# Latent attention: the 64 sample queries of two heads in one tile of 128 rows

## The chip, the cores and the metric

The kernel runs on one core of one Trainium2 chip. The metric is the device time of one execution in microseconds (us); for one core, the time of that core. The engines are TensorE (PE; its weight loads have a line of their own, PEld), VectorE (DVE), ScalarE (ACT), GpSimd (POOL) and SyncE (SP), which here only issues loads.

## What is computed

One step of a two-layer encoder over two groups of tokens: a prompt of 256 new tokens with no past, and a sample of 64 new tokens behind a cache of 128. D_MODEL is 2048, all in float32. The first layer mixes by latent attention (16 heads), the second by stick-breaking attention (16 heads); each layer is `x + W_o(mixer(RMSNorm(x)) * silu(gate))`, and a final norm follows. The change touches only the first layer's attention:

```
proj = h @ w_in                      # query latent, kv latent, rotary key, gate
q = (rms(cq) @ w_q_up): 128 plain + 64 rotary columns a head
kv = ckv_all @ w_kv_up               # per head 128 of k, 128 of v
k = [k plain, one rotary key shared by all heads]
s = q.k * 192**-0.5; masked where key chunk > query chunk (64 frames)
o = softmax(s) @ v
out = (o * silu(gate)) @ w_o
```

A sample query sees the 128 cached keys and the sample's own 64: 192 keys. A prompt query sees the prompt's keys up to the end of its own chunk: the first 128 queries at most 128 keys, the next 128 up to 256.

## The kernel before, in words

All 320 new tokens (T = 320: 256 of the prompt, then 64 of the sample, `S`) are columns of one activation, and KV = 448 adds the 128 of the cache. Weight products are made from fp32r halves: `split` (L67) casts a loaded weight tile to `hi` on ScalarE and subtracts to `lo` on VectorE, and each product is taken as hi·hi + hi·lo + lo·hi, three matmuls. `plain_split` (L148) does the same to an activation. Where a product is small, plain fp32 is used: TensorE then shows two passes for one product, with two weight loads.

The layer's input products and gates come first (to L319). Then the attention stage (L321 to L486) takes the heads in eight pairs. A pair runs: in every other pair (`even`) the rotary query products of four heads (L410 to L419); two plain query products (L423); two key products of 448 columns (L432); the rotary halves of the query, `qr`, `QA` (high and low part in one tile) and `QB` (high part with four mask rows) (L441 to L451); and four groups that make the pair's V for tokens 128 to 255, 0 to 127, the sample's own and the cache (L458 to L479). The sample's own V group has high and low latent in one 128-row tile, `own`, and adds the two halves of the result (`low`, L474).

Then the pair's heads each go through three steps, which `mla_head` (L340) returns:
- `scores` (L345): queries are the weights that stay in the array, keys stream. Prompt queries 0 to 127 against 128 keys, queries 128 to 255 against 256 keys, both into `sc`, and the sample's 64 queries against 192 keys into 64 rows of `o`. The latter are five products: three for the plain part (L358 to L360), `QA` and `QB` (L361, L362). Then for each part the maximum (L373), the exponential with its row sum (L374), reciprocals (L375, L376) and a scale (L378); p is the prompt's probabilities, `pq` the sample's.
- `transposes` (L381): five transposes into one bank `tr`; the sample's 192 columns are taken as columns 0 to 127 and 64 to 191, and `pq` has 64 rows of zeros. The first 256 columns are split into `ph`, `pl`, the others copied as `pt`.
- `values` (L394): three fp32r products for the prompt's first 128 keys (L396 to L398), then fp32 ones: keys 128 to 255 (L399), the cache's 128 keys for the sample (L400), the sample's own (L401, whose `vv` has 64 rows of zeros). The result times the gate (L403) is split into `oh`, `ol` for the output product.

The order of the work is written by hand through a queue of steps: behind each product group stands a `tick` (L61) that runs the next entry. A pair's scores of both heads are issued at once behind its V groups, and L486 queues the rest for the following groups: two empty entries, the first head's transposes, an empty one, the second head's transposes, the first head's values, the second's. So the first transposes stand behind three product groups of the next pair. After the last pair three first halves of the output product (`gemms`, L104) take the place of those groups. Within an engine's queue, instructions that are ready may have been put ahead of others when the program was built. Buffers that matter: PSUM banks `sc` 2, `o` 2, `tr` 1, `g` 3; `whi`/`wlo` 3; `QA` 4; `qr`, `og` 1.

Of the kernel before, what the change touches and what calls it, by code (L numbers as in the profile page):

```python
# [17 lines left out]
P = 128  # L18
# [17 lines left out]
def stream_encoder(  # L36
# [136 lines left out]

    def sum_bank():
        return pss.tile([P, 512], F32, name="sc")[:, :T]
# [22 lines left out]
    with ExitStack() as stack:  # L198
        mp = stack.enter_context(tc.tile_pool(name="mla", bufs=1, reuse_waits="tile"))
        with tc.tile_pool(name="mla_a", bufs=1, reuse_waits="tile") as pa:  # L200
# [66 lines left out]
            for j in range(4):  # L267
                QB = mp.tile([P, T], F32R, name=f"QB{j}")
                s.copy(QB[ROPE : ROPE + 4, :], qm[ROPE : ROPE + 4, :])
                QBs.append(QB)  # L270

# [56 lines left out]
        R = slice(0, ROPE + 4)  # L328


        pqs, vvs = [], []
        for i in range(2):
            pq = pb.tile([P, 192], F32, name=f"pq{i}")
            v.memset(pq[TS:P, :], 0.0)
            pqs.append(pq)
            vv = pb.tile([P, 3, 256], F32, name=f"vv{i}")
            v.memset(vv[TS:P, 2, :], 0.0)
            vvs.append(vv)

        def mla_head(h, qn, qh, ql, QA, QB, kn, kh, kl, vh, vl, vv, c0):  # L340

            vs = slice(c0, c0 + P)
            at = {}

            def scores():  # L345
                sc = pss.tile([P, 512], F32, name="sc")
                o = pso.tile([P, 512], F32, name="o")
                for out, q0, q1, k0, k1 in (
                    (sc[:, 0:128], 0, P, 0, P),
                    (sc[:, 128:384], P, TP, 0, TP),  # L350
                    (o[0:TS, T:512], TP, T, TP, KV),
                ):
                    q, k = slice(q0, q1), slice(k0, k1)
                    if q0 == 0:
                        pe.matmul(out, qn[:, q], kn, start=True, stop=False)
                    else:
                        q_ = slice(q0 - P, q1 - P)
                        pe.matmul(out, qh[:, q_], kh[:, k], start=True, stop=False)  # L358
                        pe.matmul(out, qh[:, q_], kl[:, k], start=False, stop=False)
                        pe.matmul(out, ql[:, q_], kh[:, k], start=False, stop=False)  # L360
                    pe.matmul(out, QA[:, q], KA[:, k], start=False, stop=False)  # L361
                    pe.matmul(out, QB[R, q], KB[R, k], start=False, stop=True)  # L362
                nm = pb.tile([P, 4], F32, name="nm", bufs=2)
                sm = pb.tile([P, 4], F32, name="sm", bufs=2)
                p = pb.tile([P, 384], F32, name="p", bufs=2)
                pq = pqs[h % 2]
                parts = (
                    (p[:, 0:128], sc[:, 0:128], P, 0),
                    (p[:, 128:384], sc[:, 128:384], P, 1),
                    (pq[0:TS, :], o[0:TS, T:512], TS, 2),  # L370
                )
                for dst, src, n, i in parts:
                    v.tensor_reduce(out=nm[:n, i : i + 1], in_=src, axis=AX.X, op=ALU.max, negate=True)  # L373
                    s.activation(dst, src, AF.Exp, bias=nm[:n, i : i + 1], accum_out=sm[:n, i : i + 1])  # L374
                v.reciprocal(sm[:, 0:2], sm[:, 0:2])  # L375
                v.reciprocal(sm[:TS, 2:3], sm[:TS, 2:3])  # L376
                for dst, src, n, i in parts:
                    v.tensor_scalar(dst, dst, sm[:n, i : i + 1], None, op0=ALU.mult)  # L378
                at.update(o=o, p=p, pq=pq)

            def transposes():  # L381
                p, pq = at["p"], at["pq"]
                tr = pst.tile([P, 512], F32, name="tr")

                for c, src in ((0, p[:, 0:P]), (P, p[:, P:TP]), (TP, pq[:, 0:P]), (T, pq[:, TS:192]), (384, p[:, TP:384])):
                    pe.transpose(tr[:, c : c + P], src, ident_t)  # L386
                ph = pb.tile([P, TP], F32R, name="ph", bufs=2)
                pl = pb.tile([P, TP], F32R, name="pl", bufs=2)
                plain_split(ph, pl, tr[:, 0:256])
                pt = pb.tile([P, 256], F32, name="pt", bufs=2)  # L390
                s.copy(pt, tr[:, 256:512])
                at.update(ph=ph, pl=pl, pt=pt)

            def values():  # L394
                o, ph, pl, pt = (at[x] for x in ("o", "ph", "pl", "pt"))
# [7 lines left out]
                v.tensor_tensor(out=og, in0=o[:, :T], in1=sg[:, h, :], op=ALU.mult)  # L403
                plain_split(oh[:, h, :], ol[:, h, :], og)
# [3 lines left out]
        for pair in range(H // 2):  # L408
# [13 lines left out]
            heads = []  # L422
            for j in range(2):  # L423
                ps = gemm_lora(whi, wlo, j, cq_h, cq_l, T)
                qn = pb.tile([P, T], F32, name="qn", bufs=2)
                qh = pb.tile([P, T - P], F32R, name="qh", bufs=2)
                ql = pb.tile([P, T - P], F32R, name="ql", bufs=2)
                v.tensor_tensor(out=qn, in0=ps, in1=rq, op=ALU.mult)
                plain_split(qh, ql, qn[:, P:T])
                heads.append([qn, qh, ql])  # L430
            whi, wlo = split(raw[:, 1024:2048], 1024)
            for j in range(2):  # L432
# [6 lines left out]
                heads[j] += [None, None, kn, kh, kl]  # L439
            x1c, x1s, x2c, x2s = ab  # L440
            for j in range(2):  # L441
                i = 2 * (pair % 2) + j
                qr = pb.tile([ROPE, T], F32, name="qr")
                rows = slice(32 * i, 32 * i + 32)
                v.tensor_tensor(out=qr[0:32, :], in0=x1c[rows, :], in1=x2s[rows, :], op=ALU.subtract)
                v.tensor_tensor(out=qr[32:64, :], in0=x1s[rows, :], in1=x2c[rows, :], op=ALU.add)
                QA = pb.tile([P, T], F32R, name="QA", bufs=4)
                s.copy(QA[0:ROPE, :], qr)
                v.tensor_tensor(out=QA[ROPE:P, :], in0=qr, in1=f32(QA[0:ROPE, :]), op=ALU.subtract)
                s.copy(QBs[i][0:ROPE, :], f32(QA[0:ROPE, :]))  # L450
                heads[j][3:5] = [QA, QBs[i]]  # L451
# [5 lines left out]
            vv = vvs[pair % 2]  # L457
            for i, t0 in ((0, P), (None, 0), (2, None), (1, T)):  # L458
# [21 lines left out]
            work = []  # L480
            for j in range(2):
                work.append(mla_head(2 * pair + j, *heads[j], vh, vl, vv, j * P))
            (s0, t0, v0), (s1, t1, v1) = work
# [267 lines left out]
```

## Time and profile before

| | us |
|---|---|
| median of 3 runs (lowest, highest) | 1100.1 (1099.86, 1100.15) |
| the profiled execution | 1099.41 |
| its span, first to last instruction | 1097.6 |
| TensorE busy | 1076.9 |
| VectorE busy | 667.8 |
| ScalarE busy | 578.5 |
| mean granted clock of TensorE, share of full speed | 0.995 |

A row of a profile names line, engine, operation and tiles as out<-in, and its time in us or ns; busy shares count an engine from the start of an instruction to its end, and matmuls overlap each other. A row of the timeline gives the start in us from the first instruction, then the length, and joins equal neighbours (x2). The layer's attention stage lies at about 183 to 370 us.

### The profile page before, as it was taken

The page shows a single profiled execution, that of the slowest core. Times are in us where ns is not written, and L with a number is a line of the kernel's source. Part 1 is how long each engine was busy: PE and PEld are TensorE (multiplying, and loading weights), DVE is VectorE, ACT ScalarE, POOL GpSimd, SP SyncE. Part 2 cuts the span into 40 slices and gives each one's busy share as a digit, 9 for nine tenths or more (in the row PEclk, how much of TensorE's full clock was granted, in tenths as well). Part 3 has the DMA queues.
Part 4 walks back from the last instruction along what each step waited for, and adds up shares of the span by engine and source line. Part 5 has one row for each costly group of instructions (what it writes and reads, how often), then busy time and mean ns, then how long its engine had stood idle before and what let it go on. Part 6 is the DMA issues. An engine that isn't in the chain of part 4 may idle for free.

```text
span 1097.6 us, 18604 instructions
## 1 busy us (share of the span) xinstructions
PE 1076.9 (98%) x7484; PEld 1070.5 (98%) x7484; DVE 667.8 (61%) x1345; ACT 578.5 (53%) x1228; POOL 18.7 (2%) x38
## 2 busy tenths in 40 slices
PE   7999999999999999999999999999999999999994
PEld 7999999999999999999999999999999999999994
DVE  7776556887887555565555555555555555554444
ACT  7755555665656444445455554544555545544441
POOL 0000000000000000000000000000000000000000
PEclk9999999999999999999999999999999999999997
DMA  9545443321322745543435444444444444434422
GB/s 310 167 159 192 154 151 99 116 97 58 116 62 73 236 174 177 174 166 127 161 125 182 133 161 138 165 151 146 133 155 148 145 154 139 157 125 154 153 78 96
DMA packets 30550, 159.39 MB, mean 145 GB/s; under 512 B 4264, under 2 KB 8304, under 8 KB 13952
## 3 DMA queue, kind: packets, MB, share of 16 engines
q1 hardware_dynamic: 26912, 151.01, 40.1%
q0 software_dynamic: 1712, 5.98, 1.5%
q10 hardware_dynamic: 1840, 1.22, 0.4%
q8 instruction: 58, 0.95, 0.4%
q14 instruction: 28, 0.23, 0.1%
HBM read 149.59 MB, written 8.60 MB: 144 GB/s over the span
## 4 chain that ended last, share of the span: by engine, by line
PE 97%; DMA 1%; DVE 1%; ACT 0%; issue 0%; DVEq 0%; SPq 0%
PE g L84 25%; PE g L87 25%; PE g L85 25%; PE g L124 2%; PE g L126 2%; PE g L125 2%; PE g L468 1%; PE g L469 1%; PE g L470 1%; PE tr L386 1%; PE sc L556 1%; DVE x L646 1%; DMA xt<-xT 1%; PE o L580 1%; PE sc L538 1%; PE tr L568 0%
## 5 line engine op out<-in xcount | busy, mean ns | idle before, releaser
L72 ACT CAST whi<-raw 128x512 fp32r<-128x512 f32 (+1 forms) x539 | 309.3, 615 | 328.4 <-PE g L85 254.9
L73 DVE TENSOR_TENSOR wlo<-raw,whi 128x512 fp32r<-128x512 f32 (+1 forms) x539 | 353.1, 682 | 129.8 <-ACT whi L72 116.4
L84 PE MATMUL g<-x2h,whi 128*128 128x320 f32 x1024 | 306.1, 313 | 0.0
L85 PE MATMUL g<-x2l,whi 128*128 128x320 f32 x1024 | 302.2, 309 | 0.0
L84 PE MATMUL g<-ah,whi 128*128 128x320 f32 x848 | 250.8, 310 | 0.0
L85 PE MATMUL g<-al,whi 128*128 128x320 f32 x848 | 250.4, 309 | 0.0
L85 PEld LDWEIGHTS g<-x2l,whi 128*128 128x128 f32 x1024 | 192.5, 188 | 0.0
L84 PEld LDWEIGHTS g<-x2h,whi 128*128 128x128 f32 x1024 | 192.5, 188 | 0.0
L87 PE MATMUL g<-x2h,wlo 128*128 128x320 f32 x1024 | 171.0, 309 | 0.0
L85 PEld LDWEIGHTS g<-al,whi 128*128 128x128 f32 x848 | 159.2, 188 | 0.1
L84 PEld LDWEIGHTS g<-ah,whi 128*128 128x128 f32 x848 | 159.1, 188 | 0.1
L87 PEld LDWEIGHTS g<-x2h,wlo 128*128 128x128 f32 x1024 | 155.4, 188 | 0.0
L87 PE MATMUL g<-ah,wlo 128*128 128x320 f32 x848 | 141.6, 309 | 0.0
L87 PEld LDWEIGHTS g<-ah,wlo 128*128 128x128 f32 x848 | 128.7, 188 | 0.0
L633 DVE TENSOR_TENSOR x<-g,x 128x320 f32<-128x320 f32 x16 | 7.9, 491 | 37.5 <-PE g L87 37.5
L124 PE MATMUL g<-cq_h,whi 128*128 128x320 f32 x96 | 30.1, 314 | 0.0
L125 PE MATMUL g<-cq_l,whi 128*128 128x320 f32 x96 | 29.7, 309 | 0.0
L126 PE MATMUL g<-cq_h,wlo 128*128 128x320 f32 x96 | 29.7, 309 | 0.0
L621 DVE TENSOR_TENSOR g<-g,r 128x320 f32<-128x320 f32 x16 | 7.9, 492 | 34.5 <-PE g L87 34.5
L609 DVE TENSOR_TENSOR kT<-g,r 128x320 f32<-128x320 f32 x16 | 7.9, 491 | 34.0 <-PE g L87 34.0
L468 PE MATMUL g<-whi,ckv_h 128*128 128x256 f32 x96 | 28.3, 295 | 0.0
L603 DVE TENSOR_TENSOR q<-g,r1s 128x320 f32<-128x320 f32 x16 | 7.9, 491 | 32.4 <-PE g L87 32.3
(267 smaller groups left out, 1384.9 us busy)
## 6 DMA issues: line engine op xcount, KB each, us to landing
raw<-wsb SPq DMA_DIRECT2D x64, 1024.0 KB, 4.8
raw<-wo SPq DMA_DIRECT2D x32, 1024.0 KB, 4.9
raw<-win SPq DMA_DIRECT2D x21, 1024.0 KB, 4.9
raw<-wmla SPq DMA_DIRECT2D x12, 1024.0 KB, 4.8
xt<-xT SPq DMA_DIRECT2D x16, 160.0 KB, 2.7
ok<-kT POOLq DMA_DIRECT2D x16, 160.0 KB, 2.4
ov<-vT POOLq DMA_DIRECT2D x16, 160.0 KB, 2.1
raw<-win SPq DMA_DIRECT2D x3, 768.0 KB, 7.4
```

The source lines that it names most:

```text
L72: s.copy(hi[:, c], raw[:, c])
L73: v.tensor_tensor(out=lo[:, c], in0=raw[:, c], in1=f32(hi[:, c]), op=ALU.subtract)
L84: pe.matmul(out, hi[:, w], xh[:, k, :], start=k == 0, stop=False)
L85: pe.matmul(out, hi[:, w], xl[:, k, :], start=False, stop=False)
L87: pe.matmul(out, lo[:, i * P : (i + 1) * P], xh[:, k, :], start=False, stop=k == KT - 1)
L124: pe.matmul(out, hi[:, w], xh[:, k, :n], start=k == 0, stop=False)
L125: pe.matmul(out, hi[:, w], xl[:, k, :n], start=False, stop=False)
L126: pe.matmul(out, lo[:, w], xh[:, k, :n], start=False, stop=k == LT - 1)
L386: pe.transpose(tr[:, c : c + P], src, ident_t)
L468: pe.matmul(out, ckv_h[:, k, ts], whi[:, w], start=k == 0, stop=False)
L469: pe.matmul(out, ckv_l[:, k, ts], whi[:, w], start=False, stop=False)
L470: pe.matmul(out, ckv_h[:, k, ts], wlo[:, w], start=False, stop=k == LT - 1)
```

## The change

Scores, softmax and transposes are written for a pair of heads rather than for a head. The sample's 64 queries of head 0 are rows 0 to 63 and those of head 1 rows 64 to 127 of one tile. For that `qh`, `ql` become fixed tiles with 256 columns whose last 128 hold the sample's queries and, at the other head's place, zeros that are written once; `QA`, `QB` and `qr` hold both heads (640 columns, ordered so that the two sample ranges are neighbours: `pair_columns`). The sample's probabilities on the sample's own keys are written as a block diagonal into the right half of `pq`, so that one product with `vo` (own V of head 0 in rows 0 to 63, of head 1 in rows 64 to 127) serves both heads; those on the cached keys are the left half. Head 0's fourth transpose takes the left half, head 1's the right. The sample's values of both heads, their gate product and split come at the end of head 1's `values`. The queue of steps keeps its entries.

```diff
+    def pair_columns():
+
+        return (slice(0, T), slice(0, T)), (slice(T, T + TS), slice(TP, T)), (slice(T + TS, 2 * T), slice(0, TP))
...
-            for j in range(4):
-                QB = mp.tile([P, T], F32R, name=f"QB{j}")
-                s.copy(QB[ROPE : ROPE + 4, :], qm[ROPE : ROPE + 4, :])
+            for j in range(2):
+                QB = mp.tile([P, 2 * T], F32R, name=f"QB{j}")
+                for c, src in pair_columns():
+                    s.copy(QB[ROPE : ROPE + 4, c], qm[ROPE : ROPE + 4, src])
...
+        qss = []
         for i in range(2):
...
+            q_ = [pb.tile([P, 2 * P], F32R, name=f"q{n}{i}") for n in ("h", "l")]
+            zero = slice(192 - TS * i, TP - TS * i)
+            for t in q_:
+                s.activation(t[:, zero], ident_t[:, :TS], AF.Copy, scale=0.0)
+            qss.append(q_)
+
+        pq = pb.tile([P, 2 * P], F32, name="pq")
+        v.memset(pq[:, P:], 0.0)
+
+        def mla_pair(pair, qns, QA, QB, ks, vh, vl, vv, vo):
+
+            at = [{}, {}]
 
             def scores():
...
+                    for out, q, n in ((sc[:, 0:P], slice(0, P), P), (sc[:, P:384], slice(P, TP), TP)):
+                        if n == P:
+                            pe.matmul(out, qns[j][:, q], kn, start=True, stop=False)
+                        else:
+                            pe.matmul(out, qh[:, 0:P], kh[:, 0:TP], start=True, stop=False)
+                            pe.matmul(out, qh[:, 0:P], kl[:, 0:TP], start=False, stop=False)
+                            pe.matmul(out, ql[:, 0:P], kh[:, 0:TP], start=False, stop=False)
+                        q = slice(q.start + j * (T + TS), q.stop + j * (T + TS))
+                        pe.matmul(out, QA[:, q], KA[:, 0:n], start=False, stop=False)
+                        pe.matmul(out, QB[R, q], KB[R, 0:n], start=False, stop=True)
...
+                out = os[:, T:512]
+                for j in range(2):
+                    _, kh, kl = ks[j]
+                    qh, ql = qss[j]
+                    for q_, k_ in ((qh, kh), (qh, kl), (ql, kh)):
+                        first = j == 0 and k_ is kh and q_ is qh
+                        pe.matmul(out, q_[:, P:], k_[:, TP:KV], start=first, stop=False)
+                both = slice(TP, TP + P)
+                pe.matmul(out, QA[:, both], KA[:, TP:KV], start=False, stop=False)
+                pe.matmul(out, QB[R, both], KB[R, TP:KV], start=False, stop=True)
+                e = mp.tile([P, T], F32, name="sil")[:, :192]
...
+                for dst, src, nm, sm in parts:
+                    v.tensor_reduce(out=nm, in_=src, axis=AX.X, op=ALU.max, negate=True)
+                    s.activation(dst, src, AF.Exp, bias=nm, accum_out=sm)
+                for dst, src, nm, sm in parts:
+                    v.reciprocal(sm, sm)
+                    if dst is not e:
+                        v.tensor_scalar(dst, dst, sm, None, op0=ALU.mult)
+                v.tensor_scalar(pq[:, 0:P], e[:, TS:], sm, None, op0=ALU.mult)
+                for j in range(2):
+                    rows = slice(TS * j, TS * j + TS)
+                    v.tensor_scalar(pq[rows, P + TS * j : P + TS * j + TS], e[rows, 0:TS], sm[rows], None, op0=ALU.mult)
+
+            def transposes(j):
+                p = at[j]["p"]
                 tr = pst.tile([P, 512], F32, name="tr")
+                more = pq[:, j * P : (j + 1) * P]
+                for i, src in enumerate((p[:, 0:P], p[:, P:TP], p[:, TP:384], more)):
+                    pe.transpose(tr[:, i * P : (i + 1) * P], src, ident_t)
...
+            def values(j):
...
-                pe.matmul(o[:, P:TP], vv[:, 0, vs], pt[:, 128:256], start=False, stop=True)
-                pe.matmul(o[:, TP:T], vv[:, 1, vs], pt[:, 64:128], start=True, stop=False)
-                pe.matmul(o[:, TP:T], vv[:, 2, vs], pt[:, 0:64], start=False, stop=True)
-                og = pb.tile([P, T], F32, name="og")
...
+                pe.matmul(o[:, P:TP], vv[:, 0, vs], pt[:, 0:P], start=False, stop=True)
+                og = pb.tile([P, TP], F32, name="og")
+                v.tensor_tensor(out=og, in0=o[:, :TP], in1=sg[:, h, :TP], op=ALU.mult)
+                plain_split(oh[:, h, :TP], ol[:, h, :TP], og)
+                if j:
+                    past = at[0]["pt"]
+                    pe.matmul(o[:, TP:384], vo, pt[:, P:], start=True, stop=False)
+                    for i in range(2):
+                        c = slice(i * TS, (i + 1) * TS)
+                        pe.matmul(
+                            o[:, TP + i * TS : TP + (i + 1) * TS], vv[:, 1, i * P : (i + 1) * P],
+                            past[:, P + i * TS : P + (i + 1) * TS], start=False, stop=i == 1,
+                        )
+                    og = pb.tile([P, TP], F32, name="og")[:, :P].rearrange("p (j t) -> p j t", j=2)
+                    both = slice(h - 1, h + 1)
+                    v.tensor_tensor(
+                        out=og, in0=o[:, TP:384].rearrange("p (j t) -> p j t", j=2), in1=sg[:, both, S], op=ALU.mult
+                    )
+                    plain_split(oh[:, both, S], ol[:, both, S], og)
...
-                plain_split(qh, ql, qn[:, P:T])
-                heads.append([qn, qh, ql])
+                qh, ql = qss[j]
+                if j == 0:
+                    plain_split(qh[:, 0:192], ql[:, 0:192], qn[:, P:T])
+                else:
+                    plain_split(qh[:, 0:P], ql[:, 0:P], qn[:, P:TP])
+                    plain_split(qh[:, 192:TP], ql[:, 192:TP], qn[:, S])
...
+            QA = pb.tile([P, 2 * T], F32R, name="QA", bufs=2)
+            QB = QBs[pair % 2]
+            qr = pb.tile([ROPE, 2 * T], F32, name="qr")
+            for i, (c, src) in enumerate(pair_columns()):
+                i = 2 * (pair % 2) + min(i, 1)
                 rows = slice(32 * i, 32 * i + 32)
...
+                v.tensor_tensor(out=qr[0:32, c], in0=x1c[rows, src], in1=x2s[rows, src], op=ALU.subtract)
+                v.tensor_tensor(out=qr[32:64, c], in0=x1s[rows, src], in1=x2c[rows, src], op=ALU.add)
+            s.copy(QA[0:ROPE, :], qr)
+            v.tensor_tensor(out=QA[ROPE:P, :], in0=qr, in1=f32(QA[0:ROPE, :]), op=ALU.subtract)
+            s.copy(QB[0:ROPE, :], f32(QA[0:ROPE, :]))
...
-                    low = pb.tile([TS, 256], F32, name="low")
-                    s.copy(low, out[TS:P, :])
-                    v.tensor_tensor(out=vv[0:TS, i, :], in0=out[0:TS, :], in1=low, op=ALU.add)
+
+                    other = pb.tile([P, P], F32, name="other")
+                    for j in range(2):
+                        rows, rest = slice(TS * j, TS * j + TS), slice(TS - TS * j, P - TS * j)
+                        s.copy(other[rows, :], out[rest, j * P : (j + 1) * P])
+                        v.tensor_tensor(out=vo[rows, :], in0=out[rows, j * P : (j + 1) * P], in1=other[rows, :], op=ALU.add)
...
```

## Rows read from the trace of the kernel before

**Rows 1.** The page's first part: busy us, share of the span, instructions.

```profile
PE 1076.9 (98%) x7484; PEld 1070.5 (98%) x7484; DVE 667.8 (61%) x1345; ACT 578.5 (53%) x1228; POOL 18.7 (2%) x38
```

**Rows 2.** The chain that ended last, by engine.

```profile
PE 97%; DMA 1%; DVE 1%; ACT 0%; issue 0%; DVEq 0%; SPq 0%
```

**Rows 3.** Busy time by stretch: from:to, length, engines, granted clock, DMA share, GB/s.

```profile
310.00:330.00 20.00, 20.00 (x144) 19.59 (x143) 18.34 (x45) 12.07 (x35) 0.00 (x0) 1.00 0.31 95
330.00:353.00 23.00, 23.00 (x179) 22.60 (x178) 17.45 (x46) 15.12 (x44) 0.00 (x0) 1.00 0.22 79
```

**Rows 4.** Line 355, all heads: ns min/median/max, first and last start.

```profile
L355 PE MATMUL sc<-kn,qn x32: 272/275/296, 200.6 to 351.5; 128*128 128x128 f32 x32
```

**Rows 5.** Timeline of TensorE, first and second transposes of a pair.

```profile
315.01 0.38 PE L386 MATMUL tr<-ident_t,p 128*128 128x128 f32 x2
315.23 0.38 PE L386 MATMUL tr<-ident_t,pq 128*128 128x128 f32 x2
...
319.75 0.38 PE L386 MATMUL tr<-ident_t,p 128*128 128x128 f32 x2
```

**Rows 6.** Timeline of TensorE, the fp32 products of one head's values.

```profile
304.61 0.39 PE L399 MATMUL o<-pt,vv 128*128 128x128 f32 x2
304.83 0.33 PE L400 MATMUL o<-pt,vv 128*128 128x64 f32 x2
305.00 0.39 PE L401 MATMUL o<-pt,vv 128*128 128x64 f32 x2
305.19 0.36 PE L468 MATMUL g<-whi,ckv_h 128*128 128x256 f32 x1
305.40 0.28 PE L469 MATMUL g<-whi,ckv_l 128*128 128x256 f32 x1
```

**Rows 7.** Timeline of TensorE's weight loads, the same products.

```profile
304.49 0.31 PEld L399 LDWEIGHTS o<-pt,vv 128*128 128x128 f32 x2
304.72 0.30 PEld L400 LDWEIGHTS o<-pt,vv 128*128 128x128 f32 x2
...
305.17 0.19 PEld L468 LDWEIGHTS g<-whi,ckv_h 128*128 128x128 f32 x1
```

**Rows 8.** Timeline of TensorE: first sample score of a head, and what follows the fifth.

```profile
309.26 0.25 PE L358 MATMUL o<-kh,qh 128*64 128x192 f32 x1
...
309.71 0.33 PE L124 MATMUL g<-cq_h,whi 128*128 128x320 f32 x1
```

**Rows 9.** Timeline of TensorE in the second layer: 192 columns behind 128-column weights.

```profile
498.80 0.25 PE L559 MATMUL sc<-sph,minusR 128*128 128x192 f32 x1
498.89 0.28 PE L559 MATMUL sc<-spl,minusR 128*128 128x192 f32 x1
```

**Rows 10.** Groups of VectorE, 201 to 353 us: busy us, mean ns; idle before.

```profile
L73 DVE TENSOR_TENSOR wlo<-raw,whi 128x512 fp32r<-128x512 f32 x50 | 33.8, 687 | 7.2 <-ACT whi L72 6.4
...
L150 DVE TENSOR_TENSOR ql<-qn,qh 128x192 fp32r<-128x192 f32 x14 | 4.9, 352 | 1.7 <-ACT qh L149 1.7
```

**Rows 11.** Timeline of VectorE through a pair's softmax.

```profile
308.11 0.28 DVE L373 TENSOR_REDUCE nm<-sc 128x1 f32<-128x128 f32 x1
308.41 0.69 DVE L73 TENSOR_TENSOR wlo<-raw,whi 128x512 fp32r<-128x512 f32 x1
...
312.36 0.34 DVE L373 TENSOR_REDUCE nm<-o 64x1 f32<-64x192 f32 x1
...
313.92 0.31 DVE L378 TENSOR_SCALAR pq<-pq,sm 64x192 f32<-64x192 f32 x1
```

**Rows 12.** Timeline of VectorE, the last split of the attention stage.

```profile
369.98 0.49 DVE L150 TENSOR_TENSOR al<-og,ah 128x320 fp32r<-128x320 f32 x1 [0.53 <-ACT ah L149]
```

**Rows 13.** Timeline of ScalarE behind the first transposes of that pair.

```profile
316.88 0.46 ACT L448 CAST QA<-qr 64x320 fp32r<-64x320 f32 x1 [2.38 <-DVE qr L445]
...
317.74 0.36 ACT L149 CAST ph<-tr 128x256 fp32r<-128x256 f32 x1
...
318.86 0.37 ACT L391 COPY pt<-tr 128x256 f32<-128x256 f32 x1 [0.51 <-DVE pl L150]
```

More of the change, by code (lines that the diff above doesn't have):

```diff
@@ L328, in stream_encoder @@
         R = slice(0, ROPE + 4)
-        pqs, vvs = [], []
+        S = slice(TP, T)
+        qss = []
         for i in range(2):
[L333 to L343, printed above, removed]
-            def scores():
[L346 to L382, printed above, removed]
@@ L388, in transposes @@
                 pl = pb.tile([P, TP], F32R, name="pl", bufs=2)
[L389 to L395, printed above, removed]
+                plain_split(ph, pl, tr[:, 0:TP])
+                pt = pb.tile([P, 2 * P], F32, name="pt", bufs=2)
+                s.copy(pt, tr[:, TP:512])
@@ L396, in values @@
+                at[j].update(ph=ph, pl=pl, pt=pt)
+            def values(j):
+                h = 2 * pair + j
+                vs = slice(j * P, (j + 1) * P)
+                if j:
+                    at[1]["o"] = pso.tile([P, 512], F32, name="o")
+                o, ph, pl, pt = (at[j][x] for x in ("o", "ph", "pl", "pt"))
                 pe.matmul(o[:, 0:TP], vh[:, vs], ph, start=True, stop=False)
@@ L421, in stream_encoder @@
             whi, wlo = split(raw[:, 0:1024], 1024)
-            heads = []
+            qns, ks = [], []
             for j in range(2):
@@ L438, in stream_encoder @@
                 s.copy(kn, ps[:, :P])
-                heads[j] += [None, None, kn, kh, kl]
+                ks.append((kn, kh, kl))
             x1c, x1s, x2c, x2s = ab
-            for j in range(2):
-                i = 2 * (pair % 2) + j
-                qr = pb.tile([ROPE, T], F32, name="qr")
-                rows = slice(32 * i, 32 * i + 32)
[L445 to L451, printed above, removed]
+            QA = pb.tile([P, 2 * T], F32R, name="QA", bufs=2)
[3 more added lines that the diff above has]
+                i = 2 * (pair % 2) + min(i, 1)
+                rows = slice(32 * i, 32 * i + 32)
+                v.tensor_tensor(out=qr[0:32, c], in0=x1c[rows, src], in1=x2s[rows, src], op=ALU.subtract)
[3 more added lines that the diff above has]
+            s.copy(QB[0:ROPE, :], f32(QA[0:ROPE, :]))
             if not even:
@@ L456, in stream_encoder @@
             vl = pb.tile([P, 256], F32R, name="vl", bufs=2)
-            vv = vvs[pair % 2]
+            vv = pb.tile([P, 2, 256], F32, name="vv", bufs=2)
+            vo = pb.tile([P, P], F32, name="vo", bufs=2)
             for i, t0 in ((0, P), (None, 0), (2, None), (1, T)):
@@ L473, in stream_encoder @@
                 elif t0 is None:
-                    low = pb.tile([TS, 256], F32, name="low")
-                    s.copy(low, out[TS:P, :])
-                    v.tensor_tensor(out=vv[0:TS, i, :], in0=out[0:TS, :], in1=low, op=ALU.add)
+                    other = pb.tile([P, P], F32, name="other")
+                    for j in range(2):
+                        rows, rest = slice(TS * j, TS * j + TS), slice(TS - TS * j, P - TS * j)
+                        s.copy(other[rows, :], out[rest, j * P : (j + 1) * P])
+                        v.tensor_tensor(out=vo[rows, :], in0=out[rows, j * P : (j + 1) * P], in1=other[rows, :], op=ALU.add)
                 else:
@@ L479, in stream_encoder @@
                 tick()
[L480 to L483, printed above, removed]
-            s0()
-            s1()
+            scores, transposes, values = mla_pair(pair, qns, QA, QB, ks, vh, vl, vv, vo)
+            scores()
+            t0, t1 = partial(transposes, 0), partial(transposes, 1)
+            v0, v1 = partial(values, 0), partial(values, 1)
             steps.extend(([], [], [t0], [], [t1], [v0], [v1]))
```

24 lines of the change are left out of this document (18 added, 6 removed).

## The prediction, made before the changed kernel had run

> **What bounds the kernel now.** I read the page's first part, then the chain that ended last, then busy time by stretch, then TensorE's own order of instructions around a pair of heads. The first says that TensorE works 1076.9 us, 98% of the span [rows 1]. The chain says that 97% of the span is followed back through TensorE alone [rows 2]. A share over the span could hide a stage with another limit, so I looked at the attention stage by itself: in a 20 us stretch that opens with rotary products TensorE is busy 20.00 us, VectorE 18.34, ScalarE 12.07; in the following 23 us TensorE again all of it, VectorE 17.45; the granted clock is 1.00, the 2.4 GHz level [rows 3]. The list of waits has no line for TensorE in this stage. So each TensorE pass that goes is time that goes, as long as VectorE, the next in line, stays hidden. The eight pairs' score blocks begin from 200.6 to 351.5 us [rows 4].
>
> One more reading decides the prices: the duration of a matmul (0.25 to 0.39 us) is a latency; what it costs is the distance from one start to the next.
>
> **Part by part, on TensorE.**
>
> *Transposes.* Before, five per head: three of p, two of the sample's small tile, whose 192 columns were taken as two overlapping slices. After, four. They start 0.22 us apart in twos, 0.11 us each [rows 5]. Two fewer per pair, eight pairs: 2 x 0.11 x 8 = **1.76 us**.
>
> *Values.* Each fp32 product here is two passes. Before, a head has three of them behind its three fp32r products, six passes: two of 128 columns (L399), four of 64 (L400, L401). They run from 304.61 to 305.19, and the product behind them takes 0.21 us to its successor where 0.12 is usual, so the six cost 0.58 + 0.09 = 0.67 us [rows 6]. The weight loads say why: two from 304.49, two from 304.72, two more, and the next at 305.17: 0.68 / 6 = 0.113 us each, whether 128 or 64 columns stream behind [rows 7]. I therefore price a pass at one weight load. After, a pair has two passes for each head's own 128 columns, two for the shared `vo` and two for each head's cached values: ten in place of twelve. 2 x 0.113 x 8 = **1.81 us**. If instead a pass costs what stands between the starts (0.22, 0.17 and 0.19 for the three lines, [rows 6]), a pair goes from 2 x 0.58 = 1.16 to 3 x 0.22 + 0.17 + 0.19 = 1.02, and the term is 0.14 x 8 = 1.1 us. That is its lower end; I take the upper, because the late start behind the group has to be paid somewhere.
>
> *Sample scores.* Before, five 192-column products per head onto 64 rows: 309.26 to 309.71, 0.45 us, 0.90 per pair [rows 8]. After, eight onto 128 rows: each head's three content products stay (the other head's columns are zeros), the two rotary and mask products are shared. No row has a run of 192-column products with 128-column weights. Bounds: L559 is two of that shape in a row, 0.09 us apart [rows 9], which makes 0.72 and a gain of 0.18 x 8 = 1.4 us; the weight loads of [rows 7] follow each other 0.113 apart, which makes 0.90 and no gain. I take **0**: in L559 only one load falls into the short distance, in a run of eight every load does.
>
> *Unchanged there:* the prompt scores, eight products per head, and the four groups that make V.
>
> The sum on TensorE is 1.76 + 1.81 = 3.6 us.
>
> **Beside it, on VectorE and ScalarE.** VectorE's work per pair: one reduction less (six to five), one scale more (six to seven), one reciprocal more, one `ql` more (head 1's low part in two pieces), two rotary pieces more (three ranges of columns, not two), one `QA` fewer but twice as wide, one add more for `vo`, one gate product and one split more for the sample's columns. That is five instructions and a reciprocal more, and some 320 columns fewer, since reductions and scales lose one 64-row tile. From a 192-column and a 512-column row, (687 - 352) / 320 = 1.05 ns a column and 0.15 us fixed [rows 10]: 6 x 0.15 - 0.34 = about +0.56 us. Hidden behind TensorE: 18.34 + 0.56 = 18.9 of the 19.5 us that such a stretch would have, and the next has 5 us free [rows 3]. ScalarE loses one exponential with its accumulator read and two rotary casts and gains four small copies; with 12 of 20 us it is covered too. The setup exchanges four memsets for one memset and four 64-column copies of zeros, in the stage's first microseconds, beside the products ahead of the first scores. Loads and their queues stay as they are.
>
> *The softmax chain.* Its last result is now needed first: the fourth transpose of head 0 reads the pair's sample tile, so it waits for all five parts, both heads. Before, six parts ran in two serial blocks, 308.11 to 313.92 + 0.31 = 314.23 [rows 11], and TensorE came to the first transposes at 315.01 [rows 5], 5.30 us behind the last score product [rows 8]. After, five sixths of 6.1 us end at 313.2 if the parts stay serial. If five independent parts overlap better, the sample's own path sets the end: reduction to last scale took 312.36 to 314.23, 1.9 us [rows 11]; from the last product's end, 309.71 + 0.25, that and two more scales end near 312.3. Cover left: 1.8 to 2.7 us; cost zero. If the cover were gone, TensorE would stand for the overrun in each pair (the third rival). Where the next pair has no rotary products the first transposes also stand behind three groups, one of them wider: more room.
>
> *The end of the stage.* The pair's sample columns come last and share one buffer with head 1's, so a product, a cast and a subtraction more follow in series before k = 14 and 15 of the output product can be read. Before, the last such write ended at 369.98 + 0.49 = 370.47 us [rows 12]. The addition is three instructions of 128 columns, some 0.8 us by the price above; TensorE has the k's of three banks to take meanwhile. So 0 to 0.8 us, and I take 0.2.
>
> So 3.6 - 0.2 = 3.4 us: the profiled execution, 1099.4 us, would be 1096.0, and since the median of the runs is 0.7 us above it, **1096.7 us** there.
>
> The Trainium skill, "TensorE: Matmul & The Clock Gate", section "Back-to-back issue gap", prices a single matmul at N/2.4 ns plus 2.5: 29 ns for 64 columns, 56 for 128, 82.5 for 192. By that rule the edit of the values is worth nothing (4 x 56 + 8 x 29 against 6 x 56 + 4 x 29), the transposes 0.9 and the scores 1.3, an estimate of 2.2 us in all, 1097.9. The spacing of 0.113 us speaks against it [rows 7].
>
> **Rivals.**
>
> *Columns set the price, not weight loads.* Then scores give 1.4, transposes 1.76 (their spacing is a row), values 1.1: 4.3 - 0.2 = 4.1 us, 1096.0. For it: the 0.09 of L559 [rows 9]. Against it: the even weight loads [rows 7]. With scores at that end and values at mine it is 5.0 - 0.2, 1095.3, the lowest that the rows give. Chance 0.10. The skill's gap rule, above, is this mechanism with other numbers.
>
> *A late eviction takes the place of the passes.* In the stretches that open with rotary products ScalarE's cast of the transposed p (317.74) stands behind the rotary casts, which waited 2.38 us for VectorE; the copy of the rest of that bank ends at 319.23 [rows 13], and TensorE needs the bank for head 1's transposes at 319.75 [rows 5]. Room: 0.5 us. With one wide `QA` the cast waits for six rotary pieces rather than two. Four more at about 0.4 us are 1.6, less 1 to 2 us that an earlier end of the softmax may return: the copy is 0 to 1.6 us later, the stall up to 1.1 us in each of three such stretches, 3.3 at most. Taking 2.2, the time is 1098.9. Against it: the order on ScalarE may put the p cast first. Chance 0.18.
>
> *Slower: the whole-pair softmax overtakes its cover.* If VectorE runs other ready work between the parts (it did so once, a 0.69 us split behind the first reduction, [rows 11]), TensorE stands before the first transposes in seven of eight pairs; the last pair has three half products behind it. It decides from 315.0 us on in that stretch, 1.8 us beyond my serial estimate; to be told apart from no change the overrun must exceed (3.4 + 2.2) / 7 = 0.8 us. With 1.2 us it is 7 x 1.2 - 3.4 = +5.0, 1105.1. Against it: four or five such splits would have to come between. Chance 0.08.
>
> *Much less goes than I say:* an order in which the fp32 passes no longer pay for their loads, or stalls of 0.2 us a pair from VectorE's added load; 3.4 less 1.6 is 1.8, 1098.3. Chance 0.09.
>
> **How the numbers follow.** Forecast 0.55, the four cases 0.10, 0.18, 0.08, 0.09. About 0.2%, 2.2 us, is what a measurement can tell from no change: faster means below 1097.9. The forecast, the columns case and a third of the late evictions lie there, 0.71; slower is the one case, 0.08; the rest, 0.21, is the same. The range reaches down to 1095.0, just under the lowest sum, and up to 1099.3; the upper half of the late evictions and the slower case, under 0.2, are left out.
>
> **What would show it.** Right: the distance from the first to the last `sc<-kn,qn`, 150.9 us before [rows 4], shrinks by 7 x 0.45 = 3.1; the sample's products stand 0.11 apart; TensorE still has no line among the waits of this stage. Late evictions: TensorE waits for ScalarE's `pt` or `ph` before the second transposes of a pair. Overtaken cover: it waits for VectorE's `pq` before the first. The sum is wrong if the eight sample products stand 0.09 apart, or if the ten fp32 passes of the values take less than their loads.

## The result, and the profile after

| | before | after |
|---|---|---|
| median of the runs, us | 1100.12 | 1109.65 |
| ratio, 95% interval | | 1.0089 (1.0076 to 1.0101) |
| span of the profiled execution, us | 1097.6 | 1107.2 |
| mean granted clock, share of full speed | 0.995 | 0.991 |

The changed kernel is 9.5 us slower; 3.4 us faster was forecast, with 1095.0 to 1099.3 us as the range. Two runs with a mean granted clock of 0.75 to 0.77 (1298.7 and 1321.3 us) are left out of every median and ratio here. In the rows below, lines are those of the changed kernel: L363 is the first prompt score, L425 the last product of a head's own values, L427 the gate product of its prompt columns, L431 the product with `vo`, L434 the cached values.

First the page's engines (as [rows 1]):

```profile
PE 1076.7 (97%) x7436; PEld 1068.9 (97%) x7436; DVE 672.1 (61%) x1390; ACT 577.5 (52%) x1226; POOL 18.7 (2%) x38
```

48 TensorE instructions are gone, as the sum said, yet its busy time is only 0.2 us less. VectorE has 4.3 us more, 0.54 per pair. Next, the score blocks, first and last start (as [rows 4]):

```profile
L363 PE MATMUL sc<-kn,qn x32: 271/273/275, 201.2 to 361.1; 128*128 128x128 f32 x32
```

From the first to the last it is now 159.9 us against 150.9: 9.0 us of the loss lie there, in the attention stage. Who waited for whom on TensorE, over the whole run (us in total, times, longest), and below it the same for its weight loads:

```profile
PE o L431 <- DVE og L427: 8.5, 4, 2.6
PE o L84 <- ACT whi L72: 7.3, 2, 5.8
PE sc L674 <- ACT sq L684: 1.1, 1, 1.1
```

```profile
PEld o L431 <- DVE og L427: 9.3, 4, 2.8
```

The second and third lines lie at the start and the end of the run, with similar ones before (5.7 and 1.1 us). The first is new: the product with `vo` waits for head 1's gate product, 2.8 us in each of three pairs and 0.9 in one (counted at its weight load; the matmul's own idle time is 0.2 us less). TensorE around one of them:

```profile
239.95 0.38 PE L425 MATMUL o<-pt,vv 128*128 128x128 f32 x2
...
241.00 0.28 PE L512 MATMUL g<-whi,ckv_l 128*128 128x256 f32 x1
243.88 0.49 PE L431 MATMUL o<-pt,vo 128*128 128x128 f32 x2 [2.60 <-DVE og L427]
244.21 0.56 PE L434 MATMUL o<-pt,vv 128*128 128x64 f32 x4
...
245.32 0.41 PE L513 MATMUL g<-wlo,ckv_h 128*128 128x256 f32 x1
245.54 0.41 PE L507 MATMUL g<-whi,own 128*128 128x256 f32 x1
```

And VectorE in that time:

```profile
241.58 0.42 DVE L427 TENSOR_TENSOR og<-o,sg 128x256 f32<-128x256 f32 x1
241.91 0.61 DVE L150 TENSOR_TENSOR kl<-g,kh 128x448 fp32r<-128x448 f32 x1
242.47 0.42 DVE L150 TENSOR_TENSOR al<-og,ah 128x256 fp32r<-128x256 f32 x1
242.81 0.68 DVE L73 TENSOR_TENSOR wlo<-raw,whi 128x512 fp32r<-128x512 f32 x1
243.41 0.41 DVE L427 TENSOR_TENSOR og<-o,sg 128x256 f32<-128x256 f32 x1
```

VectorE never stands still; it comes to head 1's gate product (243.41) when TensorE has been waiting for more than 2 us. What follows on TensorE is slow as well: products of 256 columns now start 0.22 us apart (245.32, 245.54) where 0.12 is usual. Stretches of 2 us (columns as in [rows 3]):

```profile
242.00:244.00 2.00, 0.12 (x1) 0.12 (x2) 1.97 (x5) 0.98 (x4) 0.00 (x0) 1.00 0.00 0
244.00:246.00 2.00, 2.00 (x13) 2.00 (x14) 1.82 (x5) 1.22 (x3) 0.00 (x0) 0.66 0.73 180
246.00:248.00 2.00, 2.00 (x11) 2.00 (x11) 1.25 (x4) 1.23 (x4) 0.00 (x0) 0.50 0.82 348
248.00:250.00 2.00, 2.00 (x19) 2.00 (x19) 0.60 (x3) 1.16 (x4) 0.00 (x0) 0.99 0.03 8
```

TensorE works 0.12 of 2 us, and then the granted clock falls from 1.00 to 0.50, from the 2.4 GHz level to the 1.2 GHz one. So a wait can cost more than its length. It does not always: behind the wait that ends at 290.44, of the same length, the clock stayed at 1.00, and behind the one that ends at 335.51 it fell again (0.70, 0.50, 0.95 in three stretches of 2 us):

```profile
292.00:294.00 2.00, 2.00 (x19) 2.00 (x19) 1.75 (x5) 1.56 (x6) 0.00 (x0) 1.00 0.97 410
338.00:340.00 2.00, 2.00 (x12) 2.00 (x11) 1.25 (x5) 0.73 (x3) 0.00 (x0) 0.50 0.66 279
```

The best version below has the same passes and no such wait, and its blocks run 3.8 us shorter than before; against it the changed kernel loses 9.0 + 3.8 = 12.8 us, of which 9.3 are the waits. The granted clock accounts for the rest. Its missing shares in the three stretches of 2 us behind each of the two waits are 2 x (0.34 + 0.50 + 0.01) and 2 x (0.30 + 0.50 + 0.05), an estimate of 1.7 us each: 3.4 of the other 3.5.

### The profile page after: what moved, and what is told of

Same layout as the page of the kernel before. It is cut to its first block, busy times and chain, and to the rows that moved or that the text cites. A ratio compares the mean times of both kernels' runs of the same rounds, so it can differ in the third digit from the quotient of the medians.

```text
span 1107.2 us, 18564 instructions
## 1 busy us (share of the span) xinstructions
PE 1076.7 (97%) x7436; PEld 1068.9 (97%) x7436; DVE 672.1 (61%) x1390; ACT 577.5 (52%) x1226; POOL 18.7 (2%) x38
## 4 chain that ended last, share of the span: by engine, by line
PE 91%; DVE 6%; ACT 1%; DMA 1%; issue 0%; DVEq 0%; SPq 0%; ACTq 0%
PE g L84 25%; PE g L87 25%; PE g L85 25%; DVE wlo L73 1%; PE g L124 1%; PE g L126 1%; PE g L125 1%; PE g L512 1%; PE g L513 1%; PE g L511 1%; PE sc L600 1%; DMA xt<-xT 1%; DVE x L690 1%; PE o L624 1%; PE sc L582 1%; DVE qr L490 0%
## 5 line engine op out<-in xcount | busy, mean ns | idle before, releaser
L149 ACT CAST ah<-og 128x256 fp32r<-128x256 f32 (+2 forms) x40 | 16.2, 405 | 23.4 <-DVE og L427 11.4
```

The lines of the kernel that those rows point to most:

```text
L149: s.copy(hi, src)
```

## The experiments

Theory A: the sample's products write the bank that head 1's gate product has yet to read, and VectorE is late with that read. Theory B: VectorE's added work is the trouble, wherever it shows.

**The products ahead of the gate product.**

```diff
@@ values
+                if j:
+                    past = at[0]["pt"]
+                    pe.matmul(o[:, TP:384], vo, pt[:, P:], start=True, stop=False)
+                    for i in range(2):
...
                 og = pb.tile([P, TP], F32, name="og")
                 v.tensor_tensor(out=og, in0=o[:, :TP], in1=sg[:, h, :TP], op=ALU.mult)
                 plain_split(oh[:, h, :TP], ol[:, h, :TP], og)
                 if j:
-                    past = at[0]["pt"]
-                    pe.matmul(o[:, TP:384], vo, pt[:, P:], start=True, stop=False)
...
```

> The sample's three products move ahead of head 1's gate product, so no read of the bank stands between the two groups of products. Theory A (TensorE waits because the sample's products write the bank that head 1's gate product has yet to read, and that instruction is late in VectorE's queue): the wait is gone, the granted clock stays at 1.00 in the attention stage, and the 3.6 us of passes come through: 1096.0 to 1097.0 us. Theory B (VectorE carries too much in the stretches with rotary products, and the wait only shows where it is first needed): the stall reappears at another product that needs VectorE, some 2 us in each of three or four stretches; 1103 us or more.

Measured: 1100.99 us, ratio to before 1.0009 (1.0000 to 1.0018). 8.7 us came back, neither all that A promised nor B's 1103. At the weight loads the waits that are left sum to 4.3 us, and the clock stays at 1.00 in the stage: 9.3 + 3.4 - 4.3 is 8.4 of the 8.7. TensorE's waits in the stage:

```profile
PE g L124 <- DVE qn L466: 1.5, 3, 0.5
PE g L508 <- ACT vv L525: 1.3, 3, 0.4
```

The wait for the gate product is gone, and two smaller kinds stand in its place: the next pair's key product waits for a bank that VectorE's `qn` has yet to empty, and the own-V product for one that ScalarE's copy `vv` has yet to empty. Score blocks run from 201.3 to 353.3 us here, 152.0, still 1.1 more than before. VectorE in front of one of them:

```profile
252.11 0.35 DVE L392 TENSOR_REDUCE nm<-o 128x1 f32<-128x192 f32 x1
253.04 0.16 DVE L395 RECIPROCAL sm<-sm 128x1 f32<-128x1 f32 x1 [0.58 <-ACT sil L393]
253.24 0.28 DVE L398 TENSOR_SCALAR pq<-sil,sm 128x128 f32<-128x128 f32 x1
253.44 0.51 DVE L401 TENSOR_SCALAR pq<-sil,sm 64x64 f32<-64x64 f32 x2
253.98 0.49 DVE L466 TENSOR_TENSOR qn<-g,rq 128x320 f32<-128x320 f32 x1
```

The whole-pair softmax, its last reduction and its scales, stands ahead of `qn`. Both theories hold a part: A names the wait that cost most, B says rightly that another takes its place, but not its size.

**The wait alone, in the kernel before.**

```diff
@@ values
                 og = pb.tile([P, T], F32, name="og")
+                v.tensor_tensor(out=og[:, :TP], in0=o[:, :TP], in1=sg[:, h, :TP], op=ALU.mult)
                 pe.matmul(o[:, TP:T], vv[:, 1, vs], pt[:, 64:128], start=True, stop=False)
                 pe.matmul(o[:, TP:T], vv[:, 2, vs], pt[:, 0:64], start=False, stop=True)
-                v.tensor_tensor(out=og, in0=o[:, :T], in1=sg[:, h, :], op=ALU.mult)
+                v.tensor_tensor(out=og[:, TP:T], in0=o[:, TP:T], in1=sg[:, h, TP:T], op=ALU.mult)
```

> The kernel before with nothing of the pair form, but with each head's gate product split so that the prompt's part is read from the bank before the sample's two products are written to it; one small VectorE instruction more per head. Theory A: VectorE's queue is late in the old kernel too, only nothing of TensorE asked for it; 16 waits, of up to 2.5 us in the stretches with rotary products, and a lower clock behind long ones: 1106 to 1120 us. Theory B (the lateness comes from the pair form's 0.5 us of VectorE work more per pair): waits under 0.3 us a head, below 1104 us.

Measured: 1111.40 us, 1.0105 (1.0090 to 1.0121). The line of the waits:

```profile
PE o L402 <- DVE og L401: 5.6, 3, 1.9
```

The old kernel, whose VectorE load is the lighter one, loses 11.4 us to the same order of write and read. The long waits were three, for head 0 in the pairs whose values run beside the next pair's rotary work, not sixteen; the weight loads show eight, 7.6 us in all, and behind two of the three the clock fell to 0.50. So VectorE was late before the change; nothing asked for it. The trace of before has it, where TensorE ends head 0's values and VectorE begins the gate product:

```profile
323.47 0.39 PE L401 MATMUL o<-pt,vv 128*128 128x64 f32 x2
```

```profile
325.98 0.48 DVE L403 TENSOR_TENSOR og<-o,sg 128x320 f32<-128x320 f32 x1
```

2.1 us from the end of the one (323.86) to the start of the other, and the order on VectorE in between had splits and rotary work.

**The sample's result in head 0's bank.**

```diff
@@ values
-                    past = at[0]["pt"]
+                    past, o = at[0]["pt"], at[0]["o"]
```

> The changed kernel with the sample's result in head 0's bank rather than head 1's. Theory A: the wait is then for head 0's gate product, which in the changed kernel's trace ended 1.8 us before head 1's (242.00 against 243.83 us): stalls fall from 2.8 to about 1.0 us in those stretches, and if the clock falls only behind the long ones it stays: 1099 to 1103 us. If the wait has another cause than the bank (the shared buffer of the gate product, or the order on VectorE), it stays at 2.8 us and the time at 1109.

Measured: 1102.64 us, 1.0029 (1.0017 to 1.0041). The wait follows the bank: the same line, now for head 0's read, 1.7 us at most.

```profile
PE o L431 <- DVE og L427: 5.2, 3, 1.7
```

```profile
239.25 0.38 PE L425 MATMUL o<-pt,vv 128*128 128x128 f32 x2
241.36 0.49 PE L431 MATMUL o<-pt,vo 128*128 128x128 f32 x2 [1.72 <-DVE og L427]
```

Head 0's read ends at 241.31 here, 2.06 us behind the start of head 1's last own product; in the changed kernel it was 2.05. The wait was mis-estimated (1.0 us) for another reason: in the changed kernel eight products of the next group stand between L425 and L431 on TensorE (240.09 to 241.00), some 1.0 us, and in this build none does. The clock stayed at 1.00 behind these waits.

**One product group later.**

```diff
-            steps.extend(([], [], [t0], [], [t1], [v0], [v1]))
+            steps.extend(([], [], [t0], [], [t1], [v0], [v1], [sample]))
```

(`sample` holds what stood under `if j:`.)

> The changed kernel with the sample's products and gate product one entry later in the queue of steps, so that one product group of 1.0 to 1.5 us stands between head 1's values and them. Theory A: the wait is covered by that much: stalls of 1.3 to 1.9 us instead of 2.8, and less lowering of the clock: 1101 to 1105 us. Theory B: VectorE falls as far behind, and the time stays above 1107.

Measured: 1105.76 us, 1.0060 (1.0035 to 1.0085), the single runs from 1103.9 to 1112.2; between the two theories' ranges. The waits shrank from 2.6 to 2.3 us only, and the clock fell behind one of the three:

```profile
PE o L434 <- DVE og L427: 6.9, 3, 2.3
```

```profile
239.10 0.38 PE L425 MATMUL o<-pt,vv 128*128 128x128 f32 x2
...
243.23 0.49 PE L434 MATMUL o<-pt,vo 128*128 128x128 f32 x2 [2.31 <-DVE og L427]
```

The edit adds less cover than its expectation took. Twelve products stand between the two rows here, but in the changed kernel, as built, eight of them already did: four more are 0.48 us. VectorE's order there is the same in both; it begins head 1's gate product 3.65 us behind the start of L425 here, 3.46 in the changed kernel. 0.48 less 0.19 is the 0.29 us by which the wait shrank.

**The rotary pieces on GpSimd**, on top of the products-first version, and the same in the kernel before as a control:

```diff
-                v.tensor_tensor(out=qr[0:32, c], in0=x1c[rows, src], in1=x2s[rows, src], op=ALU.subtract)
-                v.tensor_tensor(out=qr[32:64, c], in0=x1s[rows, src], in1=x2c[rows, src], op=ALU.add)
+                nc.gpsimd.tensor_tensor(out=qr[0:32, c], in0=x1c[rows, src], in1=x2s[rows, src], op=ALU.subtract)
+                nc.gpsimd.tensor_tensor(out=qr[32:64, c], in0=x1s[rows, src], in1=x2c[rows, src], op=ALU.add)
```

> The products-first version with the six rotary adds and subtractions of a pair on GpSimd instead of VectorE, some 2.2 us of VectorE's work per pair. Theory A (what is left of the loss, 4.7 us in waits of 0.6 to 0.7 us, is VectorE being behind with its queue in the stretches with rotary products): both kinds of wait go, 1096.0 to 1098.0 us. Theory C (it is the order in that queue: the pair's whole softmax stands in front of the next pair's query product, however little else there is): the wait behind the first transposes stays at about 0.65 us in three pairs, the other goes: 1098.5 to 1100 us. If GpSimd is too slow for the work, the rotary products of the scores wait for it: above 1101 us.

> Control: the kernel before with its four rotary adds and subtractions of a pair on GpSimd and nothing else. TensorE had no wait in that stage, so relief of VectorE is worth nothing: 1099.5 to 1100.7 us under every theory here; a gain would say that the later kernels' gain does not come from the pair form.

Measured: 1120.57 us, 1.0189 (1.0174 to 1.0204), and the control 1118.80, 1.0176 (1.0157 to 1.0195), which the expectation missed by 18 us. For the products-first version the last case, GpSimd too slow, has the range right, but the products that wait are not those it names. The old kernel's groups of GpSimd, then ScalarE in the new one:

```profile
L446 POOL TENSOR_TENSOR qr<-rt 32x320 f32<-32x320 f32 x16 | 18.6, 1164 | 213.9 <-DVE rt L418 213.2
L445 POOL TENSOR_TENSOR qr<-rt 32x320 f32<-32x320 f32 x16 | 16.0, 1001 | 14.0 <-DVE QA L449 13.7
```

```profile
240.70 0.72 ACT L492 CAST QA<-qr 64x640 fp32r<-64x640 f32 x1 [5.81 <-POOL qr L490]
241.33 0.36 ACT L149 CAST ph<-tr 128x256 fp32r<-128x256 f32 x1
...
242.76 0.37 ACT L413 COPY pt<-tr 128x256 f32<-128x256 f32 x1 [0.19 <-DVE pl L150]
```

An add of 320 columns takes 1.0 to 1.2 us there against 0.48 on VectorE (the 320-column `qr` rows of the kernel before). The Trainium skill, "GPSIMD Engine Reference", section "Engine selection", puts GpSimd at about half VectorE's speed for elementwise work with two inputs; the rows agree. But the length is not the whole price: the rotary cast stands on ScalarE ahead of the eviction of the transposes, and all of it waited 5.81 us. TensorE's wait for it:

```profile
PE tr L408 <- ACT pt L413: 9.0, 3, 3.0
```

That is the prediction's rival of the late eviction, brought about by another edit, and it says nothing on why VectorE is late in the changed kernel. A third run, with this and the next edit together, gave 1119.98 us, 0.6 below the run with the rotary work alone, and far from A:

> The products-first version with both reliefs, some 4.2 us of VectorE's work per pair moved. Theory A: no wait left and the 3.6 us of passes in full: 1096.0 to 1097.0 us. Theory C: as with the rotary work on GpSimd alone, within 0.5 us. If ScalarE becomes late: above that run by 1 us or more.

**The scales on ScalarE**, on top of the products-first version:

```diff
                     if dst is not e:
-                        v.tensor_scalar(dst, dst, sm, None, op0=ALU.mult)
-                v.tensor_scalar(pq[:, 0:P], e[:, TS:], sm, None, op0=ALU.mult)
+                        s.activation(dst, dst, AF.Copy, scale=sm)
+                s.activation(pq[:, 0:P], e[:, TS:], AF.Copy, scale=sm)
                 for j in range(2):
                     rows = slice(TS * j, TS * j + TS)
-                    v.tensor_scalar(pq[rows, P + TS * j : P + TS * j + TS], e[rows, 0:TS], sm[rows], None, op0=ALU.mult)
+                    s.activation(pq[rows, P + TS * j : P + TS * j + TS], e[rows, 0:TS], AF.Copy, scale=sm[rows])
```

> The products-first version with the seven scales of a pair's softmax on ScalarE instead of VectorE, some 2.0 us per pair. Theory A: VectorE is relieved by as much as with GpSimd, and both waits shrink: 1096.5 to 1099.0 us. Theory C, or ScalarE taking over as the late engine (its copy of V already stood behind a cast): 1100 to 1103 us.

Measured: **1096.15 us**, 0.9965 (0.9952 to 0.9978), 0.35% faster than the kernel before, and a little below A's range. TensorE has no wait left in the stage (0.2 us once, at a weight load). The edit takes load from VectorE and also takes away the very scales that stood ahead of `qn`; which of the two counts, this run does not tell. The score blocks, and one stretch with rotary products:

```profile
L363 PE MATMUL sc<-kn,qn x32: 272/273/274, 201.3 to 348.4; 128*128 128x128 f32 x32
```

```profile
222.00:246.00 24.00, 24.00 (x178) 23.55 (x177) 20.85 (x56) 17.14 (x48) 0.00 (x0) 1.00 0.33 111
```

147.1 us from first to last, 3.8 less than before. Not all of it is saved passes: before, head 0's five sample products (0.45 us) stand between a pair's two blocks, and now they stand behind both, so the last block comes 0.5 us sooner for that alone. The first blocks of the last pair, before and here, give seven whole pairs:

```profile
349.84 0.39 PE L355 MATMUL sc<-kn,qn 128*128 128x128 f32 x2
```

```profile
347.28 0.39 PE L363 MATMUL sc<-kn,qn 128*128 128x128 f32 x2
```

From the first block (200.62 and 201.31) that is 149.2 us before and 146.0 here, 3.3 less. And the fp32 products of head 1's values, which the sum had priced:

```profile
260.53 0.38 PE L425 MATMUL o<-pt,vv 128*128 128x128 f32 x2
260.75 0.39 PE L428 MATMUL o<-pt,vo 128*128 128x128 f32 x2
260.97 0.56 PE L431 MATMUL o<-pt,vv 128*128 128x64 f32 x4
261.34 0.36 PE L512 MATMUL g<-whi,ckv_h 128*128 128x256 f32 x1
261.54 0.28 PE L513 MATMUL g<-whi,ckv_l 128*128 128x256 f32 x1
```

**The fourth corner and the last control**: the same edit in the changed kernel with its wait kept, and in the kernel before.

> The changed kernel in its own order, the wait for head 1's gate product kept, with the seven scales on ScalarE: the fourth corner beside the changed kernel, the products-first version and the version with both. If the wait's length is VectorE's backlog, 2 us less of that backlog per pair takes as much from the 2.8 us in each of three stretches, and with it the lowering of the clock: stalls of 0.5 to 1.2 us, 1098 to 1101 us. If the length comes from the place of that product in VectorE's order whatever its load, stalls stay above 2 us: 1104 us or more.

> Control: the kernel before with its six scales of a pair on ScalarE and nothing else. TensorE had no wait to lose: 1099.3 to 1100.7 us. A gain of 2 us or more would say that the best version owes its gain to ScalarE and not to the pair form.

Measured: 1101.80 us, 1.0017 (1.0008 to 1.0027), and 1099.52, 0.9995 (0.9986 to 1.0005). The wait with VectorE relieved:

```profile
PE o L431 <- DVE og L427: 4.5, 4, 1.4
```

| median, us | scales on VectorE | scales on ScalarE |
|---|---|---|
| the kernel before | 1100.0 | 1099.5 |
| changed, gate product first | 1109.7 | 1101.8 |
| changed, products first | 1101.0 | 1096.2 |

The fourth corner lies 0.8 us above its range, with a wait between the two that were foreseen; the control lies in its range. The relief alone is worth nothing that can be told in the old kernel. In the pair form the order of gate product and products costs 8.7 us with the late VectorE and 5.6 with the relieved one, where the waits at the weight loads sum to 5.3 and the clock stays at 1.00; the relief gives 7.9 and 4.8.

## Why the prediction was wrong

The step that failed is the working of the *values*, together with "Hidden behind TensorE": it priced the ten fp32 passes and put no wait among them. In the kernel before, all of a head's products stand ahead of its gate product. In the changed one head 1's gate product reads the bank first, and the pair's sample products then write other columns of the same bank. The prediction noted that the sample's columns come last, priced that only for the end of the stage (0.2 us), and did not ask who still reads the bank. The runs showed a wait of 2.8 us in three pairs and 0.9 in one, 9.3 us, and 3.4 more behind two of them at the lower clock. That it is the bank, the run with head 0's bank shows: the wait went over to head 0's read. The Trainium skill, "PSUM — Partial Sum Buffer", section "PSUM bank collisions raise a hardware error", asks that accesses of two engines be kept apart by bank and group of 32 partitions, not by address; the wait in the trace agrees, though it doesn't show whether the chip would need it. It is the page that I ought to have held against this edit, and did not.

The second part of the step: "Hidden behind TensorE: 18.34 + 0.56 = 18.9 of the 19.5 us". The load was right (0.54 us a pair measured). The inference was not. A busy share tells whether an engine keeps up over a stretch, not how late it comes to one instruction. VectorE was 2.1 us late with gate products in the old kernel, behind work for the next pair. And the products-first run shows that a second cost was there: waits of 0.4 to 0.5 us at two places (0.6 to 0.7 at the weight loads), and no gain. Whether VectorE's added load makes them, or the place of the pair's softmax in its order, is not shown.

*The sum on TensorE* (3.6 us) was right: 3.3 us over seven whole pairs in the best version, where 7 x 0.45 = 3.1 was forecast. Summed from each start to the next, transposes give 1.5 us of it, values 1.6 and scores 0.1; the forecast for seven pairs was 1.5, 1.6 and 0. The sign that was named, the distance from the first to the last block, moved by 0.5 us more for the reason given above. The prices hold: the eight passes from 260.53 to 261.34 and the late start behind them take 0.81 + 0.08 us, 0.11 a pass whether 64 or 128 columns stream, and the sample's eight products stand 0.11 us apart in the changed kernel:

```profile
270.52 0.28 PE L383 MATMUL o<-kl,qh 128*128 128x192 f32 x1
270.64 0.27 PE L383 MATMUL o<-kh,ql 128*128 128x192 f32 x1
270.75 0.27 PE L383 MATMUL o<-kh,qh 128*128 128x192 f32 x1
270.86 0.27 PE L383 MATMUL o<-kl,qh 128*128 128x192 f32 x1
```

So the value of 0 for the scores was the right end, and the rival of columns as the price falls. The Trainium skill, "TensorE: Matmul & The Clock Gate", section "Back-to-back issue gap", gives the formula that the prediction drew on for an isolated matmul, and says that in a stream of weight loads and matmuls both set the spacing. The even 0.11 us for 64, 128 and 192 columns goes with the second, so the prediction's estimate of 2.2 us put the formula where the section does not.

*The softmax chain*: the first transposes did not wait for `pq` in any run of the pair form. The slower rival had the right engine and the wrong place: the whole-pair softmax does delay what stands behind it on VectorE, and the one that suffered was `qn` (0.5 us, products-first). *The late eviction* did not occur by itself; the GpSimd runs show its mechanism. The case of stalls from VectorE's added load came nearest in kind, with 0.2 us a pair; none of the cases held the wait that decided.

What stays open: whether another order of VectorE's instructions, chosen when the program is built, would hold the gate products early enough without moving work to ScalarE; and what decides whether the clock falls behind a wait.

## What to carry to other kernels

When instructions are regrouped, list for each accumulation bank who reads and who writes it in the new order; a write that comes after a read has that reader's lateness to pay, even for other columns. Read that lateness from the trace of before, as the time from the producer's end to the reader's start; a busy share doesn't hold it. Issue all products of a bank before its first read. And before cover is added to a wait, count in TensorE's built order what already stands there.

## What the runs showed of the hardware that I had not expected

Behind a wait of 2.8 us on TensorE the granted clock was 0.66 and 0.50 in the next two stretches of 2 us, with 256-column products 0.21 us apart instead of 0.12. Two of the changed kernel's three such waits lost 1.7 us each beyond themselves, and the one between them nothing. Over the five runs that keep this wait, by the idle time of the matmul: behind waits of 1.85 to 2.6 us the clock fell five times of nine (twice of three in the changed kernel, twice of three with the wait alone in the old one, once of three one group later), and behind those of 1.4 and 1.7 us (scales on ScalarE with the wait kept, and head 0's bank) not once of six. So the length alone does not decide it, and what does is not shown.

Four rotary operations of a pair, some 1.9 us of VectorE's work, cost the old kernel 18.9 us when GpSimd did them at 1.0 to 1.2 us each. ScalarE's cast of their result waited 29.5 us for them in all, where it had waited 10.9 for VectorE, and TensorE's transposes and values waited 8.6 us, at their weight loads, for ScalarE's copy `pt`.
